# One ring of five PSUM banks in layer 1's attention, an earlier turn of the query latents, and later sums of squares ahead of the memory attention

## The chip, the core and the metric

The kernel runs on one core of one Trainium2 chip. The metric is the device time of one execution in microseconds (us), here the median of three runs. TensorE (PE) does the matrix products and the turns (transposes through a product with an identity); its weight loads (PEld) overlap the products. VectorE (DVE), ScalarE (ACT) and GpSimd (POOL) do the rest, and SyncE (SP) issues the DMAs. PE writes into PSUM, which this kernel uses as eight banks of 128 x 512 fp32 numbers.

## The reference

A trunk of two layers over x of 512 tokens by 1024 features. Each layer is

```python
x = x + 0.5 * _swiglu(_rmsnorm(x, ffn_pre_norm[layer]), ...)
h = _rmsnorm(x, mix_norm[layer])
x = x + mixer(h, ...)          # layer 0: _even_mixer, layer 1: _mla_mixer
x = x + _memory_cross_attention(_rmsnorm(x, ...), _rmsnorm(mem, ...), ...)
x = x + 0.5 * _swiglu(_rmsnorm(x, ffn_post_norm[layer]), ...)
```

Layer 1's mixer first shrinks h to latents and then opens them into 16 heads of 96 features (64 plain, 32 rotated by position), with values of 64:

```python
c_q, c_kv, k_r = jnp.split(h @ w_in, [512, 768], axis=-1)
q = (_rmsnorm(c_q, q_lora_g) @ w_uq).reshape(b, s, 16, 96)
kv = (_rmsnorm(c_kv, kv_lora_g) @ w_ukv).reshape(b, s, 16, 128)
...                            # norms of q and k, rope on the last 32
p = jax.nn.softmax(jnp.where(causal, q @ k.T * scale, -inf))
o = (p @ v) @ w_out
```

The memory attention has 4 heads of 256 over 256 memory tokens; its queries need the root mean square of every token of x.

## The kernel before

x lies turned (features on partitions) in eight tiles of 128 x 512. The stages follow one another: feed-forward, layer 0's mixer, memory attention, feed-forward twice, layer 1's mixer (`mla_in`, then `mla_attn`), memory attention, feed-forward. Each fp32 product is split in a high and a low part and done as three products (`mm3`, lines 123 to 125). Weights come in pieces by DMA; ACT makes the high part (L112), POOL or DVE the low part (L117).

A tile scheduler sets the order on each engine from the order of the code, the waits and its own estimates. `with self.queued()` puts the PE instructions of a block right behind the last recorded one (`self.pe`); so the hand-written order holds on PE around the places of the change.

**Query and key latents.** `mla_in` makes the query latents `cq` (512 wide) token tile by token tile, then the key latents `ckv` (256 wide, with 32 rotary columns, a product of 288 columns; the loop `for t in kv`). After both, `lora` is called for `cq` and then for `ckv`: DVE makes a root and scales the latents (L642), PE turns them into `tp` (L646, two banks), ACT writes the high part `ch` (L649) and DVE the low part `cl` (L650).

**Attention.** `mla_attn` walks over heads n. For each n PE does the scores of head n in three tiles (`lg`, three banks, here S0, S1, S2), the turned weights of head n-1 (`weights`: W0 and W1, then W2, tiles `pt`), pieces of other products as filler (`take`: the projections of the next group of four heads, then the output product), and the turned queries and keys of head n+2 (`turn`, here Tq and Tk, four turns each, tiles `pt`). `pt` has two banks for all five of W0, W1, W2, Tq, Tk. A tile is free again when its reader is done: the exponentials on ACT for S0 to S2 (L871), a copy on ACT for W0 (L890), on DVE for W1 and W2 (L892), and for Tq and Tk first ACT (high part) and then DVE (low part, L88 and L788). The other three banks are two for filler (`psA`, tile `A`) and one for the values (`av`).

**Memory keys and values.** `memkv` makes keys and values of the memory in four column blocks c = 0 to 3 of four weight pieces each (tile `mm`); the keys of two heads come out of each of c = 0 and 1, and a function `fin` turns one head's keys (L1074) into tile `at` (two banks), read by ACT (`kh`) and DVE (`kl`, L1079). `stats` (four short products of `ones` with the sums of squares of x, L172, then a root on DVE) takes a tile `at` as well.

Of the kernel before, what the change touches and what calls it, by code (L numbers as in the profile page):

```python
# [14 lines left out]
P = 128  # L15
D = 1024
S = 512
# [9 lines left out]
class Trunk:  # L27
# [625 lines left out]
    def mla_in(self, p, pp, cT, krr, skr, lg, tk):  # L653
        nc, a = self.nc, self.a
        w = a["mla_w_inq"]
        cq = self.t(p, [P, NT, 512], "cq")
        ckv = self.t(p, [P, NT, 256], "ckv")
        kr = self.t(p, [P, NT, 32], "kr")
        scr = self.t(p, [P, 512], "lscr")
        s1 = self.t(p, [P, NT], "ls1")  # L660
        s2 = self.t(p, [P, NT], "ls2")
        ps = self.banks(pp, "mmmm")
        for t in self.tok_rows(ps, [(w[q], 2) for q in range(4)], 512, False):
            if t == 0:
                self.stats(pp, "tp", 2)
            nc.scalar.activation(out=cq[:, t, :], in_=ps[t](), func=AF.Copy, scale=self.rc[:, t:t + 1])
        for t in range(NT):
            nc.scalar.activation(out=scr, in_=cq[:, t, :], func=AF.Square, accum_out=s1[:, t:t + 1])
        ps = self.banks(pp, "AAmm")
        kv = self.tok_rows(ps, [(a["mla_w_inkv"][:, k0 * 288:(k0 + nk) * 288], nk)  # L670
                                for k0, nk in ((0, 3), (3, 3), (6, 2))], 288, True)
        for t in kv:
            r = self.rc[:, t:t + 1]
            nc.scalar.activation(out=ckv[:, t, :], in_=ps[t]()[:, 0:256], func=AF.Copy, scale=r)
            nc.scalar.activation(out=scr[:, 0:256], in_=ckv[:, t, :], func=AF.Square, accum_out=s2[:, t:t + 1])
            nc.scalar.activation(out=kr[:, t, :], in_=ps[t]()[:, 256:288], func=AF.Copy, scale=r)
            nc.scalar.activation(out=scr[:, 0:32], in_=kr[:, t, :], func=AF.Square, accum_out=skr[:, t:t + 1])
        self.lora(p, pp, cq, 512, s1, cT, lg, 0)
        self.lora(p, pp, ckv, 256, s2, cT, lg, 4)
        tm = self.t(p, [P, NT, 16], "krt")  # L680
        for o, (x, y, op) in enumerate((("c1", "s2", ALU.subtract), ("s1", "c2", ALU.add))):
            oo = krr[:, :, o * 16:(o + 1) * 16]
            nc.vector.tensor_tensor(out=oo, in0=kr[:, :, 0:16], in1=tk[x], op=ALU.mult)
            nc.vector.tensor_tensor(out=tm, in0=kr[:, :, 16:32], in1=tk[y], op=ALU.mult)
            nc.vector.tensor_tensor(out=oo, in0=oo, in1=tm, op=op)

    def mla_attn(self, p, pl, pp, cT, krr, skr, gqk, neg, tq, o):
# [86 lines left out]
        def turn(st, h):  # L774

            r = []
            for src, nm in ((st["qs"], "q"), (st["ks"], "k")):
                ps = self.t(pp, [P, S], "pt", bufs=2)
                for t in range(NT):
                    self.pe = nc.tensor.transpose(out=ps[0:96, t * P:(t + 1) * P], in_=src[:, t, h, :], identity=self.ident)  # L780
                hi = self.t(p, [96, S], f"{nm}Th", F32R, bufs=3)
                lo = self.t(p, [96, S], f"{nm}Tl", F32R, bufs=3)
                z = ps[0:96, :]
                if nm == "q":
                    self.split(hi, lo, z, "act", "dve")
                else:
                    nc.scalar.activation(out=hi, in_=z, func=AF.Copy, scale=gqk)
                    nc.vector.scalar_tensor_tensor(out=lo, in0=z, scalar=gqk, in1=hi.bitcast(F32), op0=ALU.mult,  # L788
                                                   op1=ALU.subtract)
                r.append((hi, lo))  # L790
            return r
# [49 lines left out]
        def scores(n, qk):  # L841

            g, h = divmod(n, G)
            (qh, ql), (kh, kl) = qk
            pb = []
            nm = self.t(p, [P, NT], "anm", bufs=2)
            if n % 2 == 0:
                self.sums = self.t(p, [P, 2, NT], "asm", bufs=2)
            sm = self.sums[:, n % 2]
            for u, blks in enumerate(((3,), (2, 0), (1,))):  # L850
                z = self.t(pp, [P, S], "lg", bufs=3)
                for x, i in enumerate(blks):
                    c0 = QA[i][1]
                    wd = (i + 1) * P
                    c = slice(i * P, wd)
                    self.mm3(z[:, c0:c0 + wd], (qh[:, c], ql[:, c]), (kh[:, 0:wd], kl[:, 0:wd]), x == 0, False)

                n_ = len(blks)
                d0 = QA[blks[0]][1] + blks[0] * P
                d = z[:, d0:d0 + n_ * P].rearrange("p (b c) -> p b c", c=P)  # L860
                self.pe = nc.tensor.matmul(d, lhsT=neg[0], rhs=neg[1][:, None, :].to_broadcast([P, n_, P]), start=False,
                                           stop=True, skip_group_check=True)
                pt = self.t(pl, [P, 512 if u < 2 else 256], f"pb{u}", bufs=2)
                for i in blks:
                    c0 = QA[i][1]
                    wd = (i + 1) * P
                    nc.vector.tensor_reduce(out=nm[:, i:i + 1], in_=z[:, c0:c0 + wd], axis=AX.X, op=ALU.max, negate=True)
                for i in blks:
                    c0 = QA[i][1]
                    wd = (i + 1) * P  # L870
                    nc.scalar.activation(out=pt[:, c0:c0 + wd], in_=z[:, c0:c0 + wd], func=AF.Exp,  # L871
                                         bias=nm[:, i:i + 1], accum_out=sm[:, i:i + 1])
                pb.append(pt)
            return pb

        def weights(pb, wT, units):

            for u in units:
                blks = ((0,), (1, 3), (2,))[u]
                ps = self.t(pp, [P, S], "pt", bufs=2)  # L880
                for j in blks:
                    c0 = KA[j][1]
                    for i in range(j, NT):
                        uu, q0 = QA[i]
                        self.pe = nc.tensor.transpose(out=ps[:, c0 + (i - j) * P:c0 + (i - j + 1) * P],
                                                      in_=pb[uu][:, q0 + j * P:q0 + (j + 1) * P], identity=self.ident)
                wd = 512 if u < 2 else 256
                w = self.t(pl, [P, wd], f"wT{u}", bufs=2)
                if u == 0:
                    nc.scalar.copy(out=w, in_=ps[:, 0:wd])  # L890
                else:
                    nc.vector.tensor_copy(out=w, in_=ps[:, 0:wd])  # L892
                wT.append(w)
# [45 lines left out]
        def ahead(n):  # L939

            if n < 15:
                normed(n + 1)
            with self.queued():
                return turn(gs[n // G], n % G)

        qk = [turn(gs[0], 0), turn(gs[0], 1)]
        pb = None
        wTs = []
        for n in range(17):
            old = pb  # L950
            if n % 2 == 0 and n:
                sums = self.sums
            if n < 16:
                with self.queued():
                    pb = scores(n, qk.pop(0))
            if old is not None:
                wT = []
                with self.queued():
                    weights(old, wT, (0, 1))
                take(FILL[n][0])  # L960
                with self.queued():
                    weights(old, wT, (2,))
                wTs.append(wT)
            if len(wTs) == 2:
                with self.queued():
                    spread = inverse(sums)
            if n < 14:
                qk.append(ahead(n + 2))
            if len(wTs) == 2:
                with self.queued():  # L970
                    rb = spread()
                take(FILL[n][1] + FILL[n][2])
                with self.queued():
                    values(n - 2, wTs, rb)
                wTs = []
            else:
                take(FILL[n][1] + FILL[n][2])
# [23 lines left out]
    def memkv(self, p, pp, l, kT, V, gqk):  # L1001
# [24 lines left out]
        for c in range(4):  # L1026
            ps = [self.t(pp, [P, 2, 256], "mm", bufs=4) for _ in range(MT)]
# [11 lines left out]
            if rm is None:  # L1039
# [4 lines left out]
                y = self.rsqrt(st[:, 0:MT], MT, 1.0 / D, EPS)  # L1044
                rm = self.t(p, [P, MT], "rm")
                nc.vector.tensor_copy(out=rm, in_=y)
            if c == 1:

                with self.queued():
                    self.stats(pp, "at", 2)  # L1050
# [208 lines left out]
```

## Time and profile before

| What | Value |
|---|---|
| median of 3 runs | 2269.89 us (2269.11 to 2270.17) |
| profiled execution | 2276.53 us |
| its span | 2274.8 us |
| PE busy | 2248.7 us (99%) |
| DVE, ACT, POOL busy | 893.8, 865.5, 1017.5 us (39%, 38%, 45%) |
| DMA | 208.60 MB, mean 92 GB/s |
| mean granted clock of PE | 0.996 |

The profiled execution is 6.64 us longer than the median of the runs. The span is the time from the first to the last instruction of the trace, 1.7 us shorter than its own execution. PE busy counts pipelined instructions whose ends are modelled. The granted clock is a share of the full level (2.4 GHz); 0.5 is the lower level (1.2 GHz).

### The profile page before, as it was taken

The numbers are of one execution on the slowest core, as the hardware profiler recorded it, in microseconds if no ns is written. First come the engines' busy times: TensorE is split into PE (matmuls) and PEld (weight loads), VectorE is DVE, ScalarE is ACT, GpSimd is POOL, SyncE is SP. The second block draws the span as 40 slices with busy tenths as digits, with TensorE's granted clock in tenths as the row PEclk, the third lists the DMA queues.
The fourth block names the chain that finished last, engine by engine and source line by source line (L and its number), as shares of the span: only waits on it lengthen the run. The fifth ranks groups of instructions, "written<-read, shape, count | busy, mean of one in ns | idle before, by whom it ended". The sixth has DMA issues, their size and how long they took to land. (4 is left out here: it accounts for less than half of the span.)

```text
span 2274.8 us, 27672 instructions
## 1 busy us (share of the span) xinstructions
PE 2248.7 (99%) x10496; PEld 1851.0 (81%) x10496; DVE 893.8 (39%) x1697; ACT 865.5 (38%) x1428; POOL 1017.5 (45%) x854
## 2 busy tenths in 40 slices
PE   9999999999999999999999999999999999999999
PEld 7888888777888888888888888887777788888887
DVE  5211223465745422123422022377667555221220
ACT  5222233456544322223322222356656443222221
POOL 5545546112143454555554555536321424545543
PEclk9999999999999999999999999999999999999999
DMA  5223323211432322332322332321113312323222
GB/s 167 87 85 116 93 84 130 84 54 54 139 107 66 93 93 84 111 93 82 113 93 83 113 96 85 99 86 56 38 37 122 121 56 93 93 83 113 93 83 94
DMA packets 67493, 208.60 MB, mean 92 GB/s; under 512 B 8608, under 2 KB 10784, under 8 KB 67360
## 3 DMA queue, kind: packets, MB, share of 16 engines
q1 hardware_dynamic: 67072, 206.52, 29.4%
q8 instruction: 83, 1.36, 0.2%
q14 instruction: 50, 0.41, 0.1%
q10 hardware_dynamic: 288, 0.30, 0.1%
HBM read 204.70 MB, written 2.10 MB: 91 GB/s over the span
## 5 line engine op out<-in xcount | busy, mean ns | idle before, releaser
L117 POOL TENSOR_TENSOR wl<-wr,wh 128x512 fp32r<-128x512 f32 (+2 forms) x752 | 941.7, 1273 | 1048.5 <-ACT wh L112 1048.1
L112 ACT CAST wh<-wr 128x1024 fp32r<-128x1024 f32 (+2 forms) x422 | 406.7, 964 | 1059.7 <-PE mm L124 573.5
L123 PE MATMUL mm<-hh,wh 128*128 128x512 f32 x1408 | 548.7, 390 | 0.0
L125 PE MATMUL mm<-hh,wl 128*128 128x512 f32 x1408 | 547.9, 389 | 0.0
L124 PE MATMUL mm<-hl,wh 128*128 128x512 f32 x1408 | 547.8, 389 | 0.0
L124 PEld LDWEIGHTS mm<-hl,wh 128*128 128x128 f32 x1408 | 264.3, 188 | 55.1
L123 PEld LDWEIGHTS mm<-hh,wh 128*128 128x128 f32 x1408 | 264.3, 188 | 54.8
L125 PEld LDWEIGHTS mm<-hh,wl 128*128 128x128 f32 x1408 | 264.3, 188 | 54.7
L123 PE MATMUL A<-ah,wh 128*128 128x512 f32 x704 | 277.4, 394 | 0.0
L125 PE MATMUL A<-ah,wl 128*128 128x512 f32 x704 | 276.0, 392 | 0.0
L124 PE MATMUL A<-al,wh 128*128 128x512 f32 x704 | 273.2, 388 | 0.0
L246 DVE TENSOR_TENSOR t<-mm,rbc 128x512 f32<-128x512 f32 x87 | 60.2, 692 | 389.3 <-PE mm L125 389.3
L279 DVE SCALAR_TENSOR_TENSOR x<-A,x 128x512 f32<-128x512 f32 x64 | 44.3, 692 | 357.7 <-PE A L125 357.7
L125 PEld LDWEIGHTS A<-ah,wl 128*128 128x128 f32 x704 | 132.1, 188 | 31.0
L124 PEld LDWEIGHTS A<-al,wh 128*128 128x128 f32 x704 | 132.1, 188 | 29.6
L123 PEld LDWEIGHTS A<-ah,wh 128*128 128x128 f32 x704 | 132.4, 188 | 26.4
L244 DVE TENSOR_TENSOR t<-mm,rbc 128x512 f32<-128x512 f32 x87 | 60.2, 692 | 190.6 <-PE mm L125 185.3
L88 DVE TENSOR_TENSOR al<-t,ah 128x512 fp32r<-128x512 f32 x88 | 84.3, 958 | 58.4 <-ACT ah L84 58.4
L123 PE MATMUL A<-hh,wh 128*128 128x512 f32 x256 | 103.8, 405 | 1.4 <-ACT hh L150 1.2
L124 PE MATMUL A<-hl,wh 128*128 128x512 f32 x256 | 101.2, 395 | 0.8 <-DVE hl L151 0.8
L125 PE MATMUL A<-hh,wl 128*128 128x512 f32 x256 | 101.1, 395 | 0.6 <-POOL wl L117 0.6
L84 ACT CAST ah<-t 128x512 fp32r<-128x512 f32 x88 | 54.6, 621 | 64.9 <-DVE t L247 64.7
(348 smaller groups left out, 2991.9 us busy)
## 6 DMA issues: line engine op xcount, KB each, us to landing
wr<-in_w_gu SPq DMA_DIRECT2D x175, 512.0 KB, 3.5
wr<-in_w_dn SPq DMA_DIRECT2D x64, 384.0 KB, 3.1
wr<-in_w_dn SPq DMA_DIRECT2D x64, 320.0 KB, 2.9
wr<-in_xmem_wkv SPq DMA_DIRECT2D x32, 512.0 KB, 3.7
wr<-in_xmem_wq SPq DMA_DIRECT2D x16, 512.0 KB, 3.5
wr<-in_xmem_wo SPq DMA_DIRECT2D x16, 512.0 KB, 3.6
wr<-in_sbg_w_zv SPq DMA_DIRECT2D x12, 512.0 KB, 3.6
wr<-in_sbg_w_qk SPq DMA_DIRECT2D x8, 512.0 KB, 3.6
```

Of the source, the lines that this page charges most:

```text
L84: nc.scalar.copy(out=hi, in_=src)
L88: e.tensor_tensor(out=lo, in0=src, in1=hi.bitcast(F32), op=ALU.subtract)
L112: nc.scalar.copy(out=hi, in_=raw)
L117: e.tensor_tensor(out=lo_[:, c], in0=raw[:, c], in1=hi[:, c].bitcast(F32), op=ALU.subtract)
L123: mm(out, lhsT=A[0], rhs=B[0], start=start, stop=False, skip_group_check=True)
L124: mm(out, lhsT=A[0], rhs=B[1], start=False, stop=False, skip_group_check=True)
L125: self.pe = mm(out, lhsT=A[1], rhs=B[0], start=False, stop=stop, skip_group_check=True)
L244: nc.vector.tensor_tensor(out=t1, in0=pg, in1=self.rbc, op=ALU.mult)
L246: nc.vector.tensor_tensor(out=t2, in0=pu, in1=self.rbc, op=ALU.mult)
L279: nc.vector.scalar_tensor_tensor(out=self.x[m], in0=ps, scalar=0.5, in1=self.x[m], op0=ALU.mult, op1=ALU.add)
```

## The change

Three edits. The turn of the query latents (`lora` of `cq`) is called inside the loop of the key latents' product, once token tile t = 1 has been read, and queued behind the PE instruction recorded last. In `mla_attn` the tiles `lg` and `pt` get one tag, `z`, with five banks: a ring in which each new tile takes the bank that was taken five tiles ago. In `memkv` (both layers) `stats` is called after column block c = 2 in place of c = 1. No instruction is added or removed; line numbers behind the first edit are three higher.

```diff
             nc.scalar.activation(out=scr[:, 0:32], in_=kr[:, t, :], func=AF.Square, accum_out=skr[:, t:t + 1])
-        self.lora(p, pp, cq, 512, s1, cT, lg, 0)
+            if t == 1:
+
+                with self.queued():
+                    self.lora(p, pp, cq, 512, s1, cT, lg, 0)
         self.lora(p, pp, ckv, 256, s2, cT, lg, 4)
@@ turn
-                ps = self.t(pp, [P, S], "pt", bufs=2)
+                ps = self.t(pp, [P, S], "z", bufs=5)
@@ scores
-                z = self.t(pp, [P, S], "lg", bufs=3)
+                z = self.t(pp, [P, S], "z", bufs=5)
@@ weights
-                ps = self.t(pp, [P, S], "pt", bufs=2)
+                ps = self.t(pp, [P, S], "z", bufs=5)
@@ memkv
-            if c == 1:
+            if c == 2:
 
                 with self.queued():
                     self.stats(pp, "at", 2)
```

**Attention, PE, the end of one head's turned weights.** The rows are PE's, of before, at a place in the second half of the head loop where the filler is a query projection (`A`): the last weights tile (W2), then Tq and Tk of a later head. In brackets stands whose event an instruction waits for.

```order
L125 MATMUL A_12715<-wh_12708,cl_2001_11298 128x384
L885 MATMUL pt_12732<-ident_114,pb_2262_12530 128x128 [waits Activation_49]
L885 MATMUL pt_12732<-ident_114,pb_2260_12519 128x128
L780 MATMUL pt_12740<-ident_114,qs_11904 96x128 [waits DVE_49]
L780 MATMUL pt_12740<-ident_114,qs_11904 96x128 x3
L780 MATMUL pt_12749<-ident_114,ks_11990 96x128 [waits DVE_49]
L780 MATMUL pt_12749<-ident_114,ks_11990 96x128 x3
L123 MATMUL A_12758<-wh_12701,ch_1994_11291 128x384
```

The same place on PE after the change:

```order
L125 MATMUL A_12715<-wh_12708,cl_2001_11298 128x384
L888 MATMUL z_12732<-ident_114,pb_2262_12530 128x128 [waits Activation_49]
L888 MATMUL z_12732<-ident_114,pb_2260_12519 128x128
L783 MATMUL z_12740<-ident_114,qs_11904 96x128 [waits Activation_49]
L783 MATMUL z_12740<-ident_114,qs_11904 96x128 x3
L783 MATMUL z_12749<-ident_114,ks_11990 96x128 [waits DVE_49]
L783 MATMUL z_12749<-ident_114,ks_11990 96x128 x3
L123 MATMUL A_12758<-wh_12701,ch_1994_11291 128x384
```

The order is the same; what the first turns wait for has moved. Counted back five tiles, Tq now waits for a copy or an exponential on ACT and Tk for DVE's copy of W1; with two banks, Tq waited for the copy of W1 and Tk for the copy of W2, which PE has only just written. In the whole of the attention one pair of scores of head 0 changes places on PE, and nothing on the other engines.

**Query latents, PE.** The rows are PE's, of before, at the end of the key latents' product (`mm`, 288 columns) and the start of the first query projection (`A`, 384 columns); `tp` are the turned latents.

```order
L125 MATMUL mm_11582<-wh_11490,hl_1965_11171 128x288
L646 MATMUL tp_11629<-ident_114,cq_11311 128x128 x4
L646 MATMUL tp_11636<-ident_114,cq_11311 128x128 x4
L123 MATMUL A_11731<-wh_11719,ch_1994_11291 128x384
L124 MATMUL A_11731<-wl_11720,ch_1994_11291 128x384
```

After the change the first eight turns stand in the last token tile of the key latents' product, whose 24 products begin 11 rows ahead of the first pair:

```order
L124 MATMUL mm_11628<-wl_11484,hh_1924_10946 128x288
L646 MATMUL tp_11571<-ident_114,cq_11311 128x128
L646 MATMUL tp_11578<-ident_114,cq_11311 128x128
L125 MATMUL mm_11628<-wh_11483,hl_1925_10947 128x288
L646 MATMUL tp_11571<-ident_114,cq_11311 128x128
L646 MATMUL tp_11578<-ident_114,cq_11311 128x128
L123 MATMUL mm_11628<-wh_11483,hh_1934_11002 128x288
L124 MATMUL mm_11628<-wl_11484,hh_1934_11002 128x288
L646 MATMUL tp_11571<-ident_114,cq_11311 128x128
L646 MATMUL tp_11578<-ident_114,cq_11311 128x128
```

So 13 products of the key latents now come behind the first pair of turns, and the query projection begins without turns right ahead of it. The other eight turns of `cq` stay inside the first query projection.

**Memory keys, PE, layer 1.** The rows are PE's, of before, where c = 1 ends: the turned keys of one head (`at`, from `tk`), five products of c = 2, and the four products of `stats`.

```order
L1074 MATMUL at_14420<-ident_114,tk_14300 128x128 x2
L1074 MATMUL at_14425<-ident_114,tk_14300 128x128 x2
L123 MATMUL mm_14497<-wh_14501,mh_2698_14146 128x512
L124 MATMUL mm_14497<-wl_14502,mh_2698_14146 128x512
L125 MATMUL mm_14497<-wh_14501,ml_2699_14147 128x512
L123 MATMUL mm_14498<-wh_14501,mh_2698_14146 128x512
L124 MATMUL mm_14498<-wl_14502,mh_2698_14146 128x512
L172 MATMUL at_14430<-ones_77,sqs_13936 128x1 x4
```

After the change the same pattern stands one block later, behind the turned keys of the third head:

```order
L1077 MATMUL at_14560<-ident_114,tk_14430 128x128 x2
L1077 MATMUL at_14565<-ident_114,tk_14430 128x128 x2
L123 MATMUL mm_14601<-wh_14605,mh_2698_14146 128x512
L124 MATMUL mm_14601<-wl_14606,mh_2698_14146 128x512
L125 MATMUL mm_14601<-wh_14605,ml_2699_14147 128x512
L123 MATMUL mm_14602<-wh_14605,mh_2698_14146 128x512
L124 MATMUL mm_14602<-wl_14606,mh_2698_14146 128x512
L172 MATMUL at_14570<-ones_77,sqs_13936 128x1 x4
```

In both, `stats` takes the bank of the first of the two `at` tiles ahead of it, and waits for DVE's `kl` of that tile. Layer 0 moves in the same way. On DVE the root of `stats` moves with it.

## Rows read from the trace of the kernel before

**Rows 1.** Page, part 1: busy us (share of the span) and instructions of each engine.

```profile
PE 2248.7 (99%) x10496; PEld 1851.0 (81%) x10496; DVE 893.8 (39%) x1697; ACT 865.5 (38%) x1428; POOL 1017.5 (45%) x854
```

**Rows 2.** Waits of PE, 1554.5 to 1720 us: total us, times, longest us.

```profile
PE pt L780 <- DVE wT L892: 4.2, 6, 1.4
PE pt L780 <- DVE qTl L88: 1.2, 1, 1.2
PE pt L780 <- DVE sqr L736: 1.1, 1, 1.1
PE pt L780 <- ACT wT L890: 1.0, 4, 0.3
```

**Rows 3.** Windows: busy us (instructions) per engine; then granted clock, DMA share, GB/s.

```profile
1554.50:1569.00 14.50, 13.34 (x89) 12.06 (x88) 11.17 (x25) 12.48 (x33) 5.52 (x6) 1.00 0.17 44
...
1612.50:1616.00 3.50, 3.50 (x14) 3.50 (x13) 1.39 (x3) 0.68 (x1) 3.50 (x7) 0.51 0.00 0
...
1766.20:1769.30 3.10, 3.10 (x9) 2.41 (x8) 3.10 (x20) 1.04 (x1) 0.00 (x0) 0.50 0.18 26
```

**Rows 4.** Timeline of PE in the attention: start, length, instruction, [idle before, releaser].

```profile
1556.37 0.61 PE L780 MATMUL pt<-ident,qs 128*96 128x128 f32 x4 [1.16 <-DVE qTl L88]
...
1570.48 0.64 PE L780 MATMUL pt<-ident,ks 128*96 128x128 f32 x4 [1.13 <-DVE wT L892]
...
1589.66 0.38 PE L885 MATMUL pt<-ident,pb 128*128 128x128 f32 x2
1590.26 0.61 PE L780 MATMUL pt<-ident,qs 128*96 128x128 f32 x4 [0.23 <-ACT wT L890]
1591.17 0.64 PE L780 MATMUL pt<-ident,ks 128*96 128x128 f32 x4 [0.29 <-DVE wT L892]
...
1608.87 0.38 PE L885 MATMUL pt<-ident,pb 128*128 128x128 f32 x2
1610.15 0.64 PE L780 MATMUL pt<-ident,qs 128*96 128x128 f32 x4 [0.90 <-DVE wT L892]
1612.14 0.77 PE L780 MATMUL pt<-ident,ks 128*96 128x128 f32 x4 [1.35 <-DVE wT L892]
...
1654.26 0.64 PE L780 MATMUL pt<-ident,ks 128*96 128x128 f32 x4 [0.20 <-DVE wT L892]
```

**Rows 5.** Timeline of DVE in the attention.

```profile
1556.15 0.74 DVE L788 SCALAR_TENSOR_TENSOR kTl<-pt,gqk,kTh 96x512 fp32r<-96x512 f32 x1
...
1567.73 0.68 DVE L892 COPY wT<-pt 128x512 f32<-128x512 f32 x1
...
1609.41 0.68 DVE L892 COPY wT<-pt 128x512 f32<-128x512 f32 x1
...
1652.61 0.68 DVE L892 COPY wT<-pt 128x512 f32<-128x512 f32 x1
```

**Rows 6.** Timeline of PE in the memory keys, layer 0 and layer 1.

```profile
617.01 1.05 PE L172 MATMUL at<-ones,sqs 128*128 128x1 f32 x8 [0.35 <-DVE kl L1079]
...
1764.02 1.05 PE L172 MATMUL at<-ones,sqs 128*128 128x1 f32 x8 [1.74 <-DVE kl L1079]
...
1778.62 0.39 PE L125 MATMUL mm<-wh,ml 128*128 128x512 f32 x1
```

**Rows 7.** Timeline of DVE behind the third head's turned keys, layer 1.

```profile
1778.12 0.88 DVE L1079 SCALAR_TENSOR_TENSOR kl<-at,gqk,kh 128x256 fp32r<-128x256 f32 x2
```

**Rows 8.** Timeline of PE at the query latents.

```profile
1518.00 0.30 PE L125 MATMUL mm<-wh,hl 128*128 128x288 f32 x1
...
1519.73 1.04 PE L646 MATMUL tp<-ident,cq 128*128 128x128 f32 x8
1522.13 0.45 PE L123 MATMUL A<-wh,ch 128*128 128x384 f32 x1 [1.36 <-ACT ch L649]
```

**Rows 9.** Timeline of DVE at the query latents.

```profile
1518.27 1.68 DVE L642 TENSOR_SCALAR cq<-cq,rs_y 128x512 f32<-128x512 f32 x4
```

**Rows 10.** Timeline of ACT: the last read of the second scores tile in one head.

```profile
1588.99 0.20 ACT L871 ACTIVATION_READ_ACCUMULATOR pb<-lg,anm 128x1 f32 x1
```

## The prediction

> **What bounds the kernel now.** The page comes first: PE is busy for 2248.7 us of the 2274.8 us span [rows 1]. The change removes no work, so all it can win is time in which PE stands still or runs at its lower clock; DVE, ACT and POOL matter only through what PE waits for. The second view is the list of PE's waits over the attention, 1554.5 to 1720 us. It is short: nearly everything stands ahead of the turns of queries and keys (L780), 4.2 + 1.2 + 1.1 + 1.0 = 7.5 us by idle time [rows 2]. The reader should see the releasers: DVE's copies of turned weights and its low part of a turned query, all of them readers of the tag with two banks. The third view is PE's timeline around these waits [rows 4]. A wait costs a little more than its idle time, since the instruction ahead of it drains first: two turns last 0.38 us there and four 0.61, so each adds 0.115; behind the two at 1589.66 Tq could have come at 1589.89, and came at 1590.26. The row says 0.23 idle, and 0.37 us were lost. The fourth view is windows with the granted clock. Behind the two waits of 0.90 and 1.35 us that end at 1612.14 the clock is 0.51 for 3.5 us; behind the wait of 1.74 us of the sums of squares at 1764.02 [rows 6] it is 0.50 for 3.1 us; behind the single 1.16 us at 1556.37 it stays at 1.00 [rows 3, 4]. So the dear waits are paid twice.
>
> **The ring of five banks, wait by wait.** Its order on PE is that of before, so each wait is compared with the one that takes its place.
>
> Head 0: the second pair's Tq waits at 1556.37 for the low part in one of two banks [rows 4]. In the ring four turned tiles fit side by side. The turns go on at once, and the limit becomes DVE's low part of the first keys, over at 1556.15 + 0.74 = 1556.89 [rows 5], which the second score product needs; before, that product stood behind eight turns (0.9 us) from 1556.37 and a first product. Of the 1.16 + 0.15 us lost I take 1.0.
>
> 1570.48: Tk waits 1.13 us for the copy of W2. In the ring it waits for the copy of W1, over at 1567.73 + 0.68 = 1568.41, before Tq begins. Gain 1.2.
>
> 1590.26 and 1591.17: Tq then waits for S1's exponentials, the last read of which ends at 1588.99 + 0.20 = 1589.19 [rows 10], 0.7 us before Tq is wanted; Tk for W1's copy, over before that. Tk starts at 1589.89 + 0.46 = 1590.35 in place of 1591.17: 0.82. The list of waits has four for ACT's copy of W0 [rows 2]; one is this, and one a repeat of this pattern a group later: 1.65 together.
>
> 1612.14: here DVE is late. Tq comes behind ACT's copy of W0, about 1609.1; Tk behind DVE's copy of W1, over at 1609.41 + 0.68 = 1610.09 [rows 5], in place of 1612.14. Gain 2.05. About 0.6 us of idle remains, which is half of the 1.16 that left the clock alone at 1556. So I take the 3.5 us at 0.51 as gone too: at full clock that work takes 1.8 to 1.9, gain 1.6.
>
> 1654.26: Tk behind W1's copy, over at 1652.61 + 0.68 = 1653.29. Gain 0.95. The copy itself stands on DVE behind maxima and a root, so the wait ahead of it stays: this is the place where DVE and not the banks sets the end.
>
> Two later heads have the rest of the four waits for ACT's copy of W0 (1.0 us, of which 0.46 stand in the pattern above): 0.27 idle, 0.4 lost each, 0.8 together. Other stalls too short for the list of waits I leave out.
>
> Waits: 1.0 + 1.2 + 1.65 + 2.05 + 0.95 + 0.8 = 7.65. With the clock 9.25, say 9.3 us. Bounds: below, half of the waits come back at the next dependency on DVE and the clock still falls, 3.9; above, all of it plus unlisted stalls of about 1 us, 10.5. I take the sum, because each new releaser that I could find in the rows is over ahead of the time at which PE wants it, or is counted.
>
> **The sums of squares.** Now they wait 1.74 us in layer 1 and 0.35 us in layer 0 for `kl` [rows 6], because DVE has a root and weight parts ahead of it; with the drain 1.9 + 0.5 = 2.4. One block later the same four products stand five products behind the third head's turns, at 1778.62 [rows 6]. There DVE's two `kl` begin at 1778.12 and take 0.88 together, so the first is over at about 1778.6 [rows 7]: a wait of 0.1 at most. The root that follows is covered: the next reader of its result is the memory attention, behind all of c = 3. So 2.3, and with no stall the 3.1 us at 0.50 in layer 1 [rows 3], where half is lost, 1.5. Sum 3.8; bounds: 2.3 if the clock falls there all the same, 4.0 with no wait left.
>
> **The turn of the query latents.** Now PE does eight turns at 1519.73 and then stands for 1.36 us until ACT's first `ch` at 1522.13 [rows 8]. After, the first pair of turns stands 13 products ahead of that, where the product at 1518.00 is now [rows 8], so 0.133 us each; DVE's scaling of the four token tiles runs from 1518.27 for 1.68 us [rows 9], so the first is there at about 1518.7, the last at 1519.95, and the pairs wait for them one after the other. That is 0.7 us of wait in a new place, with the products behind it held back, since PE takes its rows in turn. The last pair goes at 1519.95, nine products (1.2 us) follow and cover ACT's `ch`: about 0.7 us won against 1522.13. But the last key latents are now read 1.5 us later, and their own root, scaling and turns, inside the first query projection, come as much later: I give the gain back there. Sum 0, between -1.4 (the whole of 1.36 gone) and +1.4 (a second wait as long).
>
> **The sum.** 9.3 + 3.8 + 0 = 13.1 us off the profiled execution's 2276.53: 2263.4. That execution is 6.64 us above the median of the runs, and I take the same difference: 2256.8.
>
> **The rivals.**
> The clock doesn't come back. What remains at 1609 to 1610 (0.6 us), or the new waits among the latents' turns, lets the clock fall as at 1612 or 1766 [rows 3]. Each such stretch costs 1.5 or 1.6 us: one 2258.4, two 2259.9. Against it stands the full clock behind the 1.16 us at 1556. The Trainium skill speaks for it, "TensorE: Matmul & The Clock Gate", section "A second HAM failure mode: psum-queue depth-cycling": a kernel that goes round its PSUM banks in every iteration leaves PE idle for moments between groups of products, and its clock swings between the levels. A ring of five is such a round, and by that rule both stretches would stay, 2259.9; the window from 1554.5 to 1569 at 1.00 does not bear it out [rows 3].
>
> DVE is the true limit of the attention. The freed banks only let PE run up against the next thing that DVE owes it (the keys' low part, W1's copy), as at 1654. For it: four of the dear waits name DVE. Against: DVE is busy for 11.2 of 14.5 us in the fullest stretch [rows 3]. Then little of the ring's 9.3 stays, and the result is 3.8 less than before, 2266.1, inside what a measurement can tell from nothing.
>
> On the other side: ACT's exponentials come late. In the ring Tq of most heads waits for the second of the exponentials of S1, read by ACT in a queue that also makes weights' high parts. At 1590 the margin is 0.7 us [rows 4, 10]. Each us beyond it is lost in each of some eleven heads. The gain of 13.1 is eaten when the exponentials come 0.7 + 13.1 / 11 = 1.9 us later than in this row; at 2.5 us late the time is 2269.9 + 11 x 0.6 = 2276.5. The order on ACT is unchanged and its inputs come earlier, not later, so this is unlikely.
>
> **How the numbers follow.** The sum as it stands 0.68, with its own range 2254 to 2259.5 (bounds of the latents, without the second stall, and of the unlisted stalls); one or two stretches of low clock 0.18; DVE as the limit 0.09; ACT late 0.05. The range leaves out the last of these and most of the last but one: 2253 to 2263. What a measurement of this kernel tells from no change is 0.2%, 4.5 us, so faster is below 2265.4: 0.87; the same 0.09; slower 0.04.
>
> **What would show it.** In the trace of the changed kernel PE's waits in the attention should fall from 7.5 us to about 2, none for W2's copy; Tk at the place of 1612 should wait for W1's copy with about 0.6 us idle, with a clock of 1.00 behind it; Tq of head 3 to 5 should not name the exponentials. L172 in the memory keys should show no wait over 0.2 us and no low clock behind it. Between the key latents and the first query projection there should be three or four waits of 0.2 to 0.7 us in place of one of 1.36. The prediction is wrong if the clock falls at a new place, if Tk's releaser becomes an operation of DVE at later times than now, or if the first query projection waits over 1.4 us for the key latents' `ch`.

## The result and the profile after

The changed kernel takes 2257.24 us (median of 4 runs, 2256.62 to 2258.09), the kernel before in the same job 2270.03 us (4 runs): a ratio of 0.9941, 95% interval 0.9924 to 0.9958. It is faster by 12.8 us; 2256.8 was predicted. The size is right, but not every term of the sum is, as the trace shows first and the experiments then.

Part 1 of the changed kernel's page:

```profile
PE 2238.2 (99%) x10496; PEld 1846.1 (82%) x10496; DVE 905.3 (40%) x1697; ACT 863.3 (38%) x1428; POOL 1017.7 (45%) x854
```

PE's waits in the same trace from 1500 to 1765 us, which holds the latents, the attention and the memory keys (total us, times, longest):

```profile
PE A L123 <- ACT sq L761: 2.5, 1, 2.5
PE z L783 <- DVE wT L895: 1.2, 2, 0.7
PE tp L646 <- issue: 0.7, 1, 0.7
PE av L915 <- DVE arT L910: 0.6, 1, 0.6
PE at L172 <- DVE kl L1082: 0.5, 1, 0.5
PE z L123 <- ACT kTh L790: 0.3, 1, 0.3
```

Of the 7.5 us ahead of the turns [rows 2], 1.2 are left, at two places, and both now wait for the copy of W1. The timeline of PE, at the places of [rows 4]:

```profile
1548.27 0.60 PE L783 MATMUL z<-ident,ks 128*96 128x128 f32 x4
1548.71 0.60 PE L783 MATMUL z<-ident,qs 128*96 128x128 f32 x4
1549.15 0.60 PE L783 MATMUL z<-ident,ks 128*96 128x128 f32 x4
1550.07 0.67 PE L123 MATMUL z<-kTh,qTh 96*128 96x512 f32 x2 [0.32 <-ACT kTh L790]
...
1561.89 0.60 PE L783 MATMUL z<-ident,qs 128*96 128x128 f32 x4
1562.33 0.60 PE L783 MATMUL z<-ident,ks 128*96 128x128 f32 x4
...
1599.31 0.38 PE L888 MATMUL z<-ident,pb 128*128 128x128 f32 x2
1599.53 0.60 PE L783 MATMUL z<-ident,qs 128*96 128x128 f32 x4
1600.59 0.64 PE L783 MATMUL z<-ident,ks 128*96 128x128 f32 x4 [0.46 <-DVE wT L895]
...
1638.90 0.64 PE L783 MATMUL z<-ident,ks 128*96 128x128 f32 x4 [0.71 <-DVE wT L895]
```

Head 0's turns go straight on and then wait 0.32 us for the first key row; Tk at 1562.33 follows Tq with no wait; where two waits ended at 1612.14 there is one of 0.46 us. DVE's copy of W1 there runs from 1599.85 for 0.68 us, so it is over at 1600.53, and Tk starts at 1600.59:

```profile
1599.85 0.68 DVE L895 COPY wT<-z 128x512 f32<-128x512 f32 x1
```

The sums of squares answer to [rows 6, 7]; first PE's timeline, layer 0 and layer 1:

```profile
624.94 1.05 PE L172 MATMUL at<-ones,sqs 128*128 128x1 f32 x8
...
1757.80 1.05 PE L172 MATMUL at<-ones,sqs 128*128 128x1 f32 x8 [0.47 <-DVE kl L1082]
```

Then DVE's, ahead of the second:

```profile
1755.80 1.22 DVE L117 TENSOR_TENSOR wl<-wr,wh 128x1024 fp32r<-128x1024 f32 x1
1756.93 0.42 DVE L86 CAST vh<-tv 128x512 fp32r<-128x512 f32 x1
1757.27 0.87 DVE L1082 SCALAR_TENSOR_TENSOR kl<-at,gqk,kh 128x256 fp32r<-128x256 f32 x2
```

Layer 0 waits no more; layer 1 keeps 0.47 us, because `kl` stands on DVE behind a low weight part of 1.22 us and a cast. In the trace of before, DVE had stood idle for 0.70 us between that weight part and the cast; [rows 7] has the `kl` that follows:

```profile
1775.84 1.22 DVE L117 TENSOR_TENSOR wl<-wr,wh 128x1024 fp32r<-128x1024 f32 x1
1777.75 0.43 DVE L86 CAST vh<-tv 128x512 fp32r<-128x512 f32 x1 [0.70 <-ACT tv L1055]
```

PE at the query latents (an answer to [rows 8]):

```profile
1513.75 0.29 PE L124 MATMUL mm<-wl,hh 128*128 128x288 f32 x1
1514.74 0.41 PE L646 MATMUL tp<-ident,cq 128*128 128x128 f32 x2 [0.69 <-issue]
1514.90 0.38 PE L125 MATMUL mm<-wh,hl 128*128 128x288 f32 x1
...
1517.27 0.29 PE L125 MATMUL mm<-wh,hl 128*128 128x288 f32 x1
1517.40 0.34 PE L123 MATMUL A<-wh,ch 128*128 128x384 f32 x1
```

The first pair of turns waits 0.69 us. The view names no releaser; DVE's scaling of the four token tiles ran from 1514.15 for 1.67 us in this trace, so the first was there near 1514.6. The query projection at 1517.40 begins without a wait.

The clock has to be looked at apart. The windows behind the places where it had fallen in the trace of before (us busy per engine, then clock, DMA share, GB/s), in the changed kernel:

```profile
1546.30:1549.50 3.20, 3.17 (x22) 2.82 (x22) 2.66 (x7) 3.20 (x9) 3.04 (x5) 1.00 0.39 128
1600.60:1604.00 3.40, 3.40 (x21) 3.26 (x21) 3.08 (x9) 2.74 (x8) 3.24 (x6) 1.00 0.01 2
1757.80:1761.00 3.20, 3.20 (x18) 2.81 (x19) 2.41 (x6) 0.90 (x2) 2.21 (x2) 1.00 0.51 164
```

The first of them stands behind a wait of 2.5 us which the change did not touch, and the clock is 1.00 all the same. In the trace of before it was 0.50 there, and there was a stretch near 476 us as well:

```profile
472.40:479.40 7.00, 7.00 (x19) 5.33 (x20) 3.90 (x10) 4.86 (x10) 0.00 (x0) 0.51 0.15 57
1551.10:1554.50 3.40, 3.36 (x9) 2.62 (x10) 2.21 (x5) 2.15 (x6) 3.24 (x5) 0.50 0.33 116
```

Matching the two traces instruction by instruction splits the 19.9 us between their ends:

| Where | us |
|---|---|
| first products of the program, with the drift up to 460 us | 0.53 |
| low clock at 476 us, code that the change doesn't touch | 3.12 |
| low clock at 1551 us, behind an untouched wait | 1.50 |
| low clock at 1612 and at 1766 us | 1.54 + 1.58 |
| sums of squares, layer 0 and layer 1, without clock | 0.47 + 1.60 |
| query latents | 0.72 |
| ring: head 0, the other heads, without clock | 0.53 + 8.31 |

The waits make 11.6 us. The rest, 8.3 us, is the clock and the start of one execution of before, which was 6.6 us above the median of its runs.

### The profile page after: what moved, and what is told of

It is laid out like the page before. It is cut to its first block, busy times and chain, and to the rows that moved or that the text cites. A ratio compares the mean times of both kernels' runs of the same rounds, so it can differ in the third digit from the quotient of the medians.

```text
span 2254.9 us, 27673 instructions
## 1 busy us (share of the span) xinstructions
PE 2238.2 (99%) x10496; PEld 1846.1 (82%) x10496; DVE 905.3 (40%) x1697; ACT 863.3 (38%) x1428; POOL 1017.7 (45%) x854
```

## The experiments

Two theories. The first is the prediction's: waits cost their length, and the long ones cost a stretch of low clock as well. The second: the waits cost their length, while low clock belongs to an execution, falls at one place or another in some of them, and enters the median with a part only. Rival to both: the DVE work, not the banks, holds PE in the attention. Each run was timed beside the kernel before, on the same chip as the others of its set. There are three sets: the first four runs, the next four and the last four; between sets the chip differs, so runs of two sets are best compared by their distance from the kernel before.

**The kernel before again**, no edit.

> The kernel before itself, nothing edited, for its clock and a second trace. Theory 1, that stretches of low clock follow PE's longer waits: each execution has the three of layer 1 (at 1551, 1612 and 1766 us in the first trace), 4.6 us together, and the trace again has them. Theory 2, that they belong to an execution and not to a wait: the first trace, 6.6 us over the median of the runs, had them and a fourth one at 470 us, and most other executions have few; then a trace near the median shows the same waits of 2.5, 1.7 and 2.25 us with a clock of 1.00 behind most of them, and the mean clock of its runs is 0.999 or 1.000.

Measured: median 2270.95 us (11 runs); the 27 runs of before beside it have 2269.37. The windows of this second trace of before:

```profile
470.00:480.00 10.00, 9.79 (x47) 7.65 (x46) 7.92 (x18) 6.44 (x13) 0.00 (x0) 1.00 0.17 54
1548.40:1551.90 3.50, 3.50 (x13) 2.57 (x12) 2.13 (x6) 2.64 (x8) 3.34 (x6) 0.51 0.38 112
1609.00:1612.50 3.50, 3.50 (x22) 3.37 (x21) 1.53 (x4) 1.56 (x3) 3.50 (x7) 1.00 0.00 0
1760.00:1763.50 3.50, 3.50 (x10) 2.68 (x10) 3.50 (x26) 1.05 (x1) 0.00 (x0) 0.51 0.04 14
```

The reader should compare the third row with the waits ahead of it, on PE's timeline of the same trace:

```profile
1606.78 0.64 PE L780 MATMUL pt<-ident,qs 128*96 128x128 f32 x4 [0.89 <-DVE wT L892]
1608.78 0.64 PE L780 MATMUL pt<-ident,ks 128*96 128x128 f32 x4 [1.35 <-DVE wT L892]
```

They are those of [rows 4], to 0.01 us, and the clock behind them is 1.00 where it was 0.51 [rows 3]. Behind the memory keys' wait and behind the one ahead of head 0 it falls again, and at 476 it does not. The traces of all 14 runs, put together, show how often it fell:

| Idle time of PE | traces that have it | traces with a stretch at the lower level behind it |
|---|---|---|
| 2.5 us ahead of head 0 | 10 | 5: both of before, ring alone, earlier turn alone, three banks and two |
| 0.89 or 0.90, then 1.35 us, ahead of one Tq and its Tk | 5 | 3: first of before, sums alone at c = 2, sums in another bank |
| 1.74 or 1.51 us, sums of squares, layer 1 | 2 | 2: both of before |
| 0.2 to 1.21 us, sums of squares, layer 1 | 9 | 0 |
| 0.2 us near 471 us | 14 | 2: first of before, earlier turn alone |

Over the 62 timed runs of before in this study the mean clock is 0.997 in 2, 0.998 in 32, 0.999 in 27 and 1.000 in one; the medians at 0.998 and 0.999 are 2270.85 and 2268.39, the lowest time is 2267.23. So neither theory holds as stated. Nearly all stretches stand behind long waits, as the first says, but behind the same wait the clock falls in some executions and not in others, as the second says. Behind the sums' wait of 1.5 us and more it fell both times; what decides it, no run here shows.

**The ring alone.**

```diff
-                ps = self.t(pp, [P, S], "pt", bufs=2)
+                ps = self.t(pp, [P, S], "z", bufs=5)
...
-                z = self.t(pp, [P, S], "lg", bufs=3)
+                z = self.t(pp, [P, S], "z", bufs=5)
```

> The kernel before with the ring of five banks alone. Both theories: the waits of the attention fall by 7.7 us plus up to 1 us of small ones. Theory 1: 1.6 us more from the clock at 1612, so 2260.7. Theory 2: the clock gives nothing in the median, so 8.2 to 8.7 us, 2261.6.

Measured: 2259.75 us (5 runs; ratio 0.9959, interval 0.9947 to 0.9972), 9.6 us less than before; between the lowest times 8.5 us, 2258.70 against 2267.23. The waits behave as both theories said; what the medians show beyond the lowest times may be clock, and five runs don't settle it. The time is below both forecasts, nearer to the first theory's. The ring is three quarters of the gain.

**The sums of squares after c = 2 alone.**

```diff
-            if c == 1:
+            if c == 2:
```

> The kernel before with the sums of squares of x after c = 2 alone, both layers. Theory 1: 2.1 us of waits and 1.5 us of clock, 2266.4. Theory 2: 2.1 us of waits alone, 2267.9.

Measured: 2268.01 us (11 runs), 1.4 us less, ratio 0.9996, interval 0.9987 to 1.0005: no difference that is clear of noise. The median is nearer to the second theory's figure. Its waits (layer 0, none; layer 1):

```profile
PE at L172 <- DVE kl L1079: 0.5, 1, 0.5
```

The wait at c = 1 isn't of one size either: 1.74 us in the first trace of before, 1.51 in the second, 1.21 with the ring alone, 0.83 with the earlier turn alone.

**The earlier turn of the query latents alone.** Its edit is the first hunk of the change.

> The kernel before with the earlier turn of the query latents alone. By the prediction's step the gain of 0.7 us at the first query product is given back at the key latents: 2270.0. By the trace of the changed kernel it keeps 0.7 us: 2269.3. If the clock at 1551 hangs on it: 1.5 us more, 2267.8.

Measured: 2269.11 us (11 runs), 0.3 us less, ratio 0.9999, interval 0.9990 to 1.0008: the times can't tell it. In the trace, matched with the second one of before, 0.7 us are kept, with the same single wait:

```profile
PE tp L646 <- issue: 0.7, 1, 0.7
```

**Three banks and two, not a ring.**

```diff
-                ps = self.t(pp, [P, S], "pt", bufs=2)
+                ps = self.t(pp, [P, S], "pt", bufs=3)
...
-                z = self.t(pp, [P, S], "lg", bufs=3)
+                z = self.t(pp, [P, S], "lg", bufs=2)
```

> The kernel before with the same five banks, but not as a ring: three for turned tiles and weights, two for scores. If a third bank for the turned tiles is all that the ring gives, Tq and Tk wait for the copies of W0 and W1 as in the ring, and the time is that of the ring alone, 2259.8. If the sharing matters, the third scores tile of each head now has to wait for the maximum and the exponential of the first (1.4 us on DVE and ACT behind 0.9 us of products in between): about 0.7 us in each of 16 heads, 11 us given back, 2270.

Measured: 2284.13 us (5 runs; ratio 1.0062, interval 1.0048 to 1.0075), 14 us slower than before. PE's waits in the attention:

```profile
PE lg L123 <- ACT pb L871: 16.8, 16, 2.7
```

All waits ahead of the turns are gone, and each of 16 heads waits 0.56 to 2.65 us, 1.05 in the mean, for the exponential of its first scores tile. The expectation had 2270: it put this wait at 0.7 us, and the clock at nothing. In this trace the clock is near 0.5 for 17.4 us of the attention, from three of these waits on:

```profile
1606.20:1613.20 7.00, 6.26 (x24) 6.26 (x25) 3.78 (x14) 2.64 (x9) 4.23 (x8) 0.51 0.14 55
1620.00:1623.40 3.40, 3.40 (x17) 3.40 (x16) 1.12 (x2) 1.60 (x7) 0.00 (x0) 0.50 0.00 0
1654.00:1661.00 7.00, 5.48 (x20) 4.79 (x21) 4.63 (x17) 3.34 (x10) 3.38 (x6) 0.51 0.23 76
```

So a third bank for turned tiles takes away their waits, but the scores need theirs as well: the ring lends a bank to either side in turn.

**A ring of four**, the changed kernel otherwise (three such lines).

```diff
-                z = self.t(pp, [P, S], "z", bufs=5)
+                z = self.t(pp, [P, S], "z", bufs=4)
```

> The changed kernel with a ring of four banks. Counted back four tiles, Tq waits for the exponential of S2, W1 for that of S0 of the same head, and the next S0 for the copy of W1. If the ring has slack to spare: within 1 us of the changed kernel, 2257. If each tile is needed, as the prediction's margin of 0.7 us for Tq says: 0.3 to 0.5 us in each of 16 heads, 2262 to 2265.

Measured: 2262.55 us (5 runs; ratio to before 0.9969, interval 0.9956 to 0.9981), 4.4 to 5.3 us over the two medians of the changed kernel in other sets. Tq, by whose margin the loss was forecast for each of 16 heads, does not wait. What waits, in seven of the 16 steps, is W1, for the exponential of the same step's S0. The expectation had counted that dependency back as well, but had not put its loss there:

```profile
PE z L888 <- ACT pb L874: 4.8, 7, 1.8
```

**The sums of squares behind c = 1, in another bank**, the kernel before otherwise.

```diff
-                    self.stats(pp, "at", 2)
+                    self.stats(self.pA, "A")
```

> The kernel before with the sums of squares of x left behind c = 1, but in a bank of the filler's pool, which nothing holds there. If the bank's reader (kl on DVE) is the wait, no wait is left in either layer: 0.5 + 1.7 to 1.9 us, 2267.0, and 0.5 us better than moving them to c = 2. If what is won there comes back, because PE runs up against the weight parts of the next block, the time is that of before, 2269.4.

Measured: 2267.22 us (11 runs; ratio 0.9988, interval 0.9979 to 0.9997), 2.9 us less than before beside it, where the later place had given 1.4 in its own set. The trace lists no wait of the sums in either layer, so the bank was the wait. That a free bank does better than a later place is likely, but these two intervals overlap.

**Four tiles of squares**, on the changed kernel, against its longest wait. The tiles `s1` and `s2`, two of tag `sq`, come in turn from `sq` and from a tag of two more:

```diff
+        def sqr4():
+
+            count[0] += 1
+            if count[0] % 4 < 2:
+                return self.t(self.sp, [P, S], "sq", bufs=2).rearrange("p (g d) -> p g d", g=G)
+            return self.t(p, [P, 384], "sqa", bufs=2).rearrange("p (g d) -> p g d", g=G)
```

> The changed kernel with four tiles instead of two for the squares of queries and keys in the first projections (ACT writes, DVE sums), against the longest wait that the change leaves, 2.5 us of PE ahead of the first head. If the two tiles are what ACT waits for: 2.3 to 2.6 us less than the changed kernel, 2254.7. If DVE is the limit there all the same, the wait moves to the first turned keys or their low part: within 0.5 us of 2257.2.

Measured: 2258.30 us (5 runs), no gain. The wait of 2.5 us is gone, and these stand in its place on PE (the releasers are ACT and DVE of head 0's turned rows):

```profile
1547.21 0.50 PE L123 MATMUL z<-kTh,qTh 96*128 96x512 f32 x1 [0.32 <-ACT kTh L798]
1549.31 0.44 PE L123 MATMUL z<-kTh,qTh 96*128 96x384 f32 x1 [1.60 <-DVE qTl L88]
1549.97 0.80 PE L124 MATMUL z<-kTl,qTh 96*128 96x512 f32 x1 [0.21 <-DVE kTl L799]
```

Here the rival holds: DVE is the limit ahead of head 0. The second scores tile takes the bank of head 0's turned queries, whose low part DVE delivers late. In this trace the clock falls behind it, too (0.51 to 0.52 from 1549.6 to 1556.6 us).

**The changed kernel again.**

> The changed kernel, nothing edited, for the clock of its runs and a second trace. If low clock belongs to executions and falls less often where PE waits less: mean clock 0.999 or 1.000, at most one stretch in the trace, a median of 2257 to 2258, and a gain between the lowest times of the two kernels of 10.5 to 11.5 us, which is that of the waits alone. If the waits alone make the gain, the lowest times differ by as much as the medians.

Measured: 2258.19 us (5 runs; ratio 0.9952, interval 0.9939 to 0.9964), lowest 2256.78. Over its nine runs the clock is 1.000 in 3, 0.999 in 5, 0.998 in one. From median to median the change gives 11.9 us in this set and 12.8 in that of the result; between the lowest times of all sets it gives 10.6, in this set alone 11.3. Matched as above, the second traces of both kernels lie 14.25 us apart, 3.15 of it in two stretches of low clock of before: 11.1 without clock, where the first two traces gave 11.6. So of the gain in the medians some 0.3 to 2 us are clock; that is an estimate from these differences. The sums waited 0.9 us in this trace, 0.5 in the first.

**Two key norms on GpSimd**, on the changed kernel.

```diff
-            eng = nc.vector if g == 0 else nc.gpsimd
+            eng = nc.vector if n < 2 else nc.gpsimd
```

> The changed kernel with the norms of the third and fourth key heads of the first group on GpSimd, not on DVE. If DVE is what holds PE ahead of the first head (in the run with four tiles of squares the wait of 2.5 us only moved to the low part of the first turned queries): DVE is 3.7 us of work ahead there, PE's wait of 2.5 us falls to 0.5 or less, 2255.2. If GpSimd, which then does them behind its own norms of queries, hands them on late: a wait at the turns of the third head, up to 3 us, and 2257 or more.

Measured: 2254.89 us (5 runs; ratio to before 0.9938, interval 0.9925 to 0.9952), 3.3 us under the changed kernel in the same set. On PE the wait shrank to

```profile
1544.27 0.50 PE L123 MATMUL A<-wh,ch 128*128 128x512 f32 x1 [0.30 <-ACT sq L761]
```

and no turn of the third head waits. So it was DVE's work that held PE there.

**The same, with the sums of squares in the other bank.** The edit is the one shown above, on c = 1.

> The run before with the sums of squares of x back behind c = 1, in a bank of the filler's pool. The 0.64 us that the sums still cost in the changed kernel go: 0.6 us less than the run before, 2254.6. If PE runs into the weight parts of the next block instead: the same as the run before.

Measured: 2253.80 us (5 runs, 2253.69 to 2253.84), 1.1 us less, 0.6 between the lowest times; the wait of the sums is gone.

**The same, with four tiles of squares.**

> The run before with four tiles of squares as well. With DVE free, PE's rest of the wait ahead of the first head goes too: 0.5 us less than the run before, 2254.1. If the limit is then the ACT chain of turned queries and keys, no change.

Measured: 2253.13 us (5 runs; ratio to before 0.9927, interval 0.9915 to 0.9940), 0.7 us less, and 5.1 us under the changed kernel of the same set: the fastest version. Tiles that gave nothing while DVE was late give their part once it isn't. PE's waits from 1500 to 1765 us are down to four:

```profile
PE z L791 <- DVE wT L903: 1.1, 2, 0.6
PE tp L646 <- issue: 0.7, 1, 0.7
PE av L923 <- DVE arT L918: 0.6, 1, 0.6
PE z L123 <- ACT kTh L798: 0.3, 1, 0.3
```

In the last two versions the mean clock is 1.000 in nine of ten runs, in the one ahead of them in two of five. Five runs lie within 0.15 us of each other in the first of the two.

## Why the prediction was right

**The ring.** Its releasers were named rightly, and so were the sizes of the large waits: 1.30, 1.99 and 0.91 us came where 1.2, 2.05 and 0.95 were set, 1.80 for 1.65 and 0.93 for 0.8 at the short ones. Head 0 gave 0.53 and not 1.0, since PE now stands for the first key's high part on ACT, a step that the sum had left out. The stalls "too short for the list" gave 1.34: six times 0.2, one with each pair of heads. Without clock 8.8 us, against 7.65. The bounds of this term, 3.9 and 10.5, should read 3.8 and 10.3; the range does not hang on it.

**The clock.** This step was mis-sized. The prediction took 3.1 us for two stretches at the lower level, as if every execution had them; the fall follows a wait only in some executions, and the trace that was read had four stretches, two of them at places that the change leaves alone. In the medians some 0.3 to 2 us of the gain are clock. The error was to read a share of 0.996 in one execution as the kernel's, with the sign in sight: that execution was 6.6 us over the median, and the text carried the difference along instead of asking for its place. Of the Trainium skill's page "TensorE: Matmul & The Clock Gate", the section "A second HAM failure mode: psum-queue depth-cycling" had stood for the rival that a round of banks keeps the clock swinging. These runs don't bear it out: with the ring the mean clock went up, from 0.998 or less in 34 of 62 runs of before to 0.999 or 1.000 in eight of nine of the changed kernel.

**The sums of squares.** The wait left in layer 1 was put at 0.1 us at most; it was 0.47, and 0.9 in the second trace. In the trace of before the low weight part ahead of `kl` was long over and DVE had stood idle for 0.70 us. After the change PE is 21.4 us earlier ahead of the moved sums, and that weight part only 20.0 us, so `kl` comes right behind it. So a row of the old trace gave the place of a neighbour on another engine that didn't move along with PE. Without clock 2.07 us, against 2.3; the run of that edit alone is not clear of noise.

**The query latents.** Set at 0 with bounds of 1.4 us on either side; 0.7 us were kept. The wait for the scaling came with the length worked out (0.69 us), as one wait and not as three or four, and so did the gain at the query projection, which begins at 1517.40 and not at 1522.13 [rows 8], 0.6 us more than the 4.12 that the traces lie apart by then; but it was kept, and the give-back assumed at the key latents did not come. Only the traces show this, since the time of that edit alone can't tell it from nothing.

**The rivals.** ACT's exponentials came late nowhere in the ring of five; in the ring of four they did, at the turned weights. DVE as the limit was wrong for most of the heads, where banks were short. It was right for what is left at two Tk (0.46 and 0.71 us for W1's copy), which the ring's sum had allowed for, and ahead of head 0, where the change had no part.

So the mechanism of the waits was right and their size somewhat low: 9.95 us in the sum, 11.1 to 11.6 in the traces. The clock's 3.1 us was too high for the medians by about as much. That 13.1 came so near to 12.8 is in part luck: one error stood in for the other.

## What to carry to other kernels

Where PE waits for a bank, list for each tile which one it takes the bank from and when that one's reader is done; a ring over tiles of two kinds lends a bank where a fixed split of the same number makes one side wait (here 9.6 us slower with three banks for the scores, and some 24 us, part of it clock, with two). When a buffer is added and the wait only moves to an engine's next result, take work off that engine first, and try the buffer again. A stretch of low clock in one trace is a sample: look at the clock of several runs before its cost goes into a sum.

## What the runs showed of the hardware

The clock fell behind one and the same wait in one execution and not in another: 0.51 and 1.00 behind 0.90 + 1.35 us of idle (it fell in three of five traces), 0.50 and 1.00 behind 2.5 us (in five of ten). Behind the sums of squares it fell after 1.74 and 1.51 us, and in none of nine traces with 0.2 to 1.21 us; but it did not fall behind the two waits of 1.8 us in the ring of four. At 476 us it fell in two of 14 traces, with the same instructions and 0.2 us of idle ahead. In the two traces of before a stretch behind a wait cost 1.5 to 1.6 us.

In the three versions where PE's waits from 1500 to 1765 us were all under 1 us, the mean clock was 1.000 in 11 of 15 runs; of the kernel before it was so in one of 62. The times of each of the last two versions agree to 0.7 us, where the kernel before scatters over 6.
